# Half-size products for six of eleven tile pairs in a feed-forward, and one list of products with factors made ahead

## The chip, the cores and the metric

The kernel runs on one core of one Trainium2 chip. The metric is the device time of one execution in microseconds (us). A core has TensorE (PE in the profile, with its weight loads as a row PEld of their own), VectorE (DVE), ScalarE (ACT), GpSimd (POOL) and SyncE (SP), which here issues the DMAs of the weights. Each engine takes its instructions in order and waits for others by semaphores.

## The reference

Two layers on 512 tokens of width 1024: differential attention in the first, sliding-window attention with sinks in the second, and in each a feed-forward with a gate (hidden width 2816):

```python
def swiglu(h, w_gate_up, w_down):
    g, u = jnp.split(h @ w_gate_up, 2, axis=-1)
    return (jax.nn.silu(g) * u) @ w_down
...
        x = x + swiglu(rms_norm(x, ffn_norm[l]), w_gate_up[l], w_down[l])
```

Inputs, weights and the result are float32.

## The kernel before

**Numbers in two parts.** TensorE multiplies a rounded format at full rate. Each factor is therefore split into a rounded part `hi` (a ScalarE copy) and the rest `lo` (a VectorE subtraction), and each product is three matmuls, hi x hi, hi x lo and lo x hi (`mm3`, L283 to L286; L585 in the down projection). Splits of gate and up weights are lines L262 and L263, those of the down weights L566 and L567; they land in rings of 8 buffers of 512 columns (`HLB`).

**The feed-forward** (class `Ffn`) holds tokens as columns: the transposed, normalized input `hT` is [128, 8 blocks, 512 tokens], again in two parts. The hidden width is cut into 11 tiles of 256 (`q`), each with a gate half and an up half of two inner tiles of 128. `start` does tile 0 in two halves of 256 tokens, since tokens 256 to 511 are transposed only then. `up(q)` does the others: four accumulations (two inner tiles, gate and up) over 8 blocks, 96 matmuls of 512 columns. `gate` applies silu and multiplies; `left` forms four sums of the gated tile and splits all seven left factors.

**The down projection** already uses seven products instead of eight: over the two halves of tokens, of inner tiles and of output columns. `right` forms four sums of a tile's down weights; `down` takes 2 or 3 tiles (chunks (0,1), (2,3,4), (5,6,7), (8,9,10)) and runs 7 products x 2 blocks of 128 tokens x tiles x 3 matmuls of 512 columns. After each product VectorE adds its bank to `xs`, the residual (L594).

**Order.** PE's order is the program's. For ScalarE, VectorE and SP a planner sets a fixed order when the kernel is built: it goes through time with estimated durations and takes, of what is ready, the first by priority, which is the place in the program, moved forward inside `tc.high_priority(offset=...)`. A tile of a ring can be written only when its last reader is done. SBUF is shared by pools: attention (`da`, `sw`) and feed-forward (`ffn0`, `ffn1`) take turns on the same space, and a tile of the later pool waits for the tiles of the earlier one under it. PSUM has eight banks of 512 columns: four `acc`, three `tr`, one `po`.

## Time and profile before

| what | us |
| --- | --- |
| median of three runs | 1165.65 (1164.84 to 1165.97) |
| the profiled execution, its own time | 1164.51 |
| its span, first to last instruction | 1162.6 |
| PE busy in the span | 1136.0 |
| VectorE busy | 841.5 |
| ScalarE busy | 583.9 |

In the lines of the profile a row names the kernel's line, the engine, the operation and output<-inputs by the program's names. Groups give the count, the total busy time and the mean of one in ns; a timeline gives start and duration in us, with the idle time before in brackets and what ended it; a table by stage gives, for a stretch of the span, each engine's busy time and number of instructions, then the granted TensorE clock, the share of time that the DMA engines were busy, and GB/s.

### The profile page before, as it was taken

To read this page: it belongs to the slowest core of one execution; us is meant where nothing else is said; L and a number is where in the kernel's file an instruction comes from. 1 tells how busy PE (TensorE), PEld (TensorE's weight loads), DVE (VectorE), ACT (ScalarE), POOL (GpSimd) and SP (SyncE) were. 2 spreads that over 40 slices of the span, in tenths; PEclk is the share of its full clock that TensorE was granted. 3 is DMA by queue.
4 is the path that set the end of the run, shared out by engine and by line. 5 is a ranking of instruction groups with operands and counts; after the bars stand their busy time and mean duration, and the time that the engine had idled before them with its cause. 6 is when DMAs were issued, how large, how long until landed. Compare 5 with 4: busy or idle time off the path is not lost.

```text
span 1162.6 us, 16451 instructions
## 1 busy us (share of the span) xinstructions
PE 1136.0 (98%) x5942; PEld 952.5 (82%) x5942; DVE 841.5 (72%) x2052; ACT 583.9 (50%) x1211; POOL 16.5 (1%) x32
## 2 busy tenths in 40 slices
PE   8999999999999999999999999989999999999998
PEld 6878888779888888888888888768988888888887
DVE  5979798978785486476467797987777567468546
ACT  6565756544433343343346579787443343343332
POOL 0100000000000000000002000000000000000000
PEclk9999999999999999999999999999999999999999
DMA  6312112124343134215203221021605206205301
GB/s 191 109 55 74 55 56 67 44 73 158 97 128 126 37 117 146 64 54 182 91 1 94 73 74 55 19 73 34 220 12 188 91 1 217 91 18 181 109 1 73
DMA packets 86579, 103.15 MB, mean 89 GB/s; under 512 B 5161, under 2 KB 68034, under 8 KB 86498
## 3 DMA queue, kind: packets, MB, share of 16 engines
q1 hardware_dynamic: 86064, 100.97, 27.2%
q0 software_dynamic: 384, 1.11, 0.4%
q8 instruction: 47, 0.77, 0.3%
q14 instruction: 34, 0.28, 0.1%
q10 hardware_dynamic: 50, 0.01, 0.0%
HBM read 99.98 MB, written 2.10 MB: 88 GB/s over the span
## 4 chain that ended last, share of the span: by engine, by line
PE 78%; DVE 14%; ACT 5%; DMA 2%; issue 1%; SPq 0%; DVEq 0%; ACTq 0%
PE acc L284 18%; PE acc L286 18%; PE acc L285 18%; PE acc L585 15%; PE tr L585 3%; DVE lo L263 1%; ACT s L1124 1%; DVE hss L377 1%; DVE s L799 1%; PE tr L795 1%; DVE u L393 1%; ACT s L1131 1%; PE po L285 1%; PE tr L302 1%; DMA raw<-in_da_w_qkv_dram 1%
## 5 line engine op out<-in xcount | busy, mean ns | idle before, releaser
L284 PE MATMUL acc<-hTh,hi 128*128 128x512 f32 (+1 forms) x768 | 285.5, 372 | 0.0
L285 PE MATMUL acc<-hTl,hi 128*128 128x512 f32 (+1 forms) x768 | 285.3, 371 | 0.0
L286 PE MATMUL acc<-hTh,lo 128*128 128x512 f32 (+1 forms) x768 | 285.1, 371 | 0.0
L262 ACT CAST hi<-raw 128x512 fp32r<-128x512 f32 x256 | 154.6, 620 | 256.3 <-PE acc L285 119.2
L263 DVE TENSOR_TENSOR lo<-raw,hi 128x512 fp32r<-128x512 f32 x256 | 172.6, 686 | 100.9 <-ACT hi L262 100.7
L566 ACT CAST hi<-g 128x512 fp32r<-128x512 f32 x154 | 95.6, 622 | 160.9 <-PE acc L285 99.4
L285 PEld LDWEIGHTS acc<-hTl,hi 128*128 128x128 f32 x768 | 144.7, 188 | 25.3 <-DVE hTl L291 0.2
L284 PEld LDWEIGHTS acc<-hTh,hi 128*128 128x128 f32 x768 | 144.6, 188 | 24.9
L286 PEld LDWEIGHTS acc<-hTh,lo 128*128 128x128 f32 x768 | 144.6, 188 | 24.9
L567 DVE TENSOR_TENSOR lo<-g,hi 128x512 fp32r<-128x512 f32 x154 | 104.6, 688 | 70.7 <-ACT hi L566 70.7
L284 PE MATMUL acc<-hi,hTh 128*128 128x256 f32 (+1 forms) x384 | 137.5, 358 | 4.9 <-ACT hTh L290 1.6
L286 PE MATMUL acc<-hi,hTl 128*128 128x256 f32 (+1 forms) x384 | 130.1, 339 | 0.3 <-DVE hTl L291 0.2
L285 PE MATMUL acc<-lo,hTh 128*128 128x256 f32 (+1 forms) x384 | 129.6, 337 | 0.4 <-DVE lo L263 0.4
L585 PE MATMUL acc<-hi,al 128*128 128x512 f32 x264 | 103.0, 390 | 0.1
L585 PE MATMUL acc<-hi,ah 128*128 128x512 f32 x264 | 102.9, 390 | 0.0
L585 PE MATMUL acc<-lo,ah 128*128 128x512 f32 x264 | 102.7, 389 | 0.0
L284 PEld LDWEIGHTS acc<-hi,hTh 128*128 128x128 f32 x384 | 72.9, 190 | 15.7 <-issue 3.7
L286 PEld LDWEIGHTS acc<-hi,hTl 128*128 128x128 f32 x384 | 72.7, 189 | 9.4 <-DVE hTl L640 0.7
L285 PEld LDWEIGHTS acc<-lo,hTh 128*128 128x128 f32 x384 | 73.0, 190 | 5.7 <-DVE lo L263 0.7
L594 DVE TENSOR_TENSOR xs<-xs,acc 128x512 f32<-128x512 f32 (+1 forms) x98 | 65.6, 671 | 8.1 <-PE acc L585 6.4
L505 DVE TENSOR_TENSOR sg<-sg,acc 128x512 f32<-128x512 f32 x44 | 30.1, 685 | 53.3 <-PE acc L286 53.3
L585 PEld LDWEIGHTS acc<-hi,al 128*128 128x128 f32 x264 | 49.5, 188 | 11.1 <-DVE al L523 0.9
(210 smaller groups left out, 1784.7 us busy)
## 6 DMA issues: line engine op xcount, KB each, us to landing
raw<-in_w_gate_up_dram SPq DMA_DIRECT2D x88, 512.0 KB, 3.5
g<-in_w_down_dram SPq DMA_DIRECT2D x88, 256.0 KB, 5.1
raw<-in_da_w_qkv_dram SPq DMA_DIRECT2D x30, 256.0 KB, 3.0
raw<-in_da_w_qkv_dram SPq DMA_DIRECT2D x8, 512.0 KB, 3.5
raw<-in_da_w_o_dram SPq DMA_DIRECT2D x8, 512.0 KB, 3.6
raw<-in_sw_w_q_dram SPq DMA_DIRECT2D x8, 512.0 KB, 3.5
raw<-in_sw_w_o_dram SPq DMA_DIRECT2D x8, 512.0 KB, 3.5
raw<-in_w_kv_dram SPq DMA_DIRECT2D x4, 512.0 KB, 3.7
```

What stands on the lines that cost most here:

```text
L262: nc.scalar.copy(hi, part)
L263: nc.vector.tensor_tensor(lo, part, hi.bitcast(F32), op=ALU.subtract)
L284: nc.tensor.matmul(dst, sh, mh, start=start, stop=False)
L285: nc.tensor.matmul(dst, sh, ml, start=False, stop=False)
L286: nc.tensor.matmul(dst, sl, mh, start=False, stop=stop)
L302: nc.tensor.transpose(pt[:, j * P:(j + 1) * P], src[:, k * P:(k + 1) * P], ident)
L377: nc.vector.tensor_reduce(out=ss[:, t, :], in_=sq.rearrange("p (g e) -> p g e", e=HD), axis=AX.X, op=ALU.add)
L505: nc.vector.tensor_tensor(sg, sg, pu, op=ALU.mult)
L566: nc.scalar.copy(hi, src)
L567: nc.vector.tensor_tensor(lo, src, hi.bitcast(F32), op=ALU.subtract)
L585: nc.tensor.matmul(bank[t], l[:, left, tk], r, start=fresh and i == 0 and n == 0, stop=i == len(qs) - 1 and n == 2, skip_group_check=not f ...
L594: nc.vector.tensor_tensor(xs[:, tok, cs], xs[:, tok, cs], bank[t][:, c0:c0 + w], op=ALU.add)
```

## The change

Six tiles (`FAST`: 2, 3, 5, 6, 8, 9) get their gate and up halves from seven half-size products each (`up7`), over the halves of the contraction (blocks 0 to 3 and 4 to 7), of the tokens and of the inner tiles. A product is 4 blocks x 3 matmuls of 256 columns, once for gate and once for up. Four sums of weights per tile are formed on VectorE (`sums12` and two more in `make`), four sums of token blocks once per layer (`tokens`). Banks are read while they go on accumulating: ScalarE copies a partial sum out, VectorE adds later ones to it.

All of a feed-forward after `start` is one list of steps (`Flow`). Each step names the split factors that it uses; a factor is written into the program four places before the step that needs it (`AHEAD`), for `up`, `up7` and `down` alike. The left factors are no longer split as a whole in `left`: seven pairs of 256 columns a tile come from a ring of five (`ah`, `al`). The right sums are formed in place beside the split of the first two right factors. Gate and up weights are loaded into three buffers of 1 MB in the feed-forward's pool (`r`) rather than into the two of 512 KB that all stages share (`raw`), which now hold the weight sums. The rotary tables `Cd` and `Sd` move from the constants' pool to that of the first attention, and the pads of the feed-forward pools go.

```diff
--- before.py
+++ after.py
+FAST = (2, 3, 5, 6, 8, 9)
+AHEAD = {'w': 4, 'a': 4}
+AHB = 5
+WRAW = 3
+XDB = 0
...
+    class Flow:
+        def __init__(self, rings):
+            self.size = rings
+            self.preps, self.steps, self.last = [], [], []
+            self.rings = {r: [] for r in rings}
+        def prep(self, ring, fn, after=-1):
+            order = self.rings[ring]
+            held = order[-self.size[ring]] if len(order) >= self.size[ring] else None
+            order.append(len(self.preps))
+            self.preps.append((fn, held, after))
+            self.last.append(None)
+            return ring, len(order) - 1
+        def step(self, fn, *uses):
+            for ring, k in uses:
+                self.last[self.rings[ring][k]] = len(self.steps)
+            self.steps.append((fn, uses))
+            return len(self.steps) - 1
+        def run(self):
+            made, goal = {r: 0 for r in self.rings}, {r: -1 for r in self.rings}
+            for i, (fn, uses) in enumerate(self.steps):
+                for ring, k in uses:
+                    goal[ring] = max(goal[ring], k + AHEAD[ring])
+                for ring, order in self.rings.items():
+                    while made[ring] < len(order) and made[ring] <= goal[ring]:
+                        make, held, after = self.preps[order[made[ring]]]
+                        if held is not None and (self.last[held] is None or self.last[held] >= i) or after >= i:
+                            break
+                        make()
+                        made[ring] += 1
+                assert all(k < made[ring] for ring, k in uses)
+                fn()
...
+        def gate(self, dst, pg, pu):
+            with tc.high_priority(offset=HOT):
+                nc.scalar.activation(dst, pg, AF.Silu)
+                nc.vector.tensor_tensor(dst, dst, pu, op=ALU.mult)
...
+        def left(self, q):
+            z = self.lf[q]
             tt = nc.vector.tensor_tensor
...
+            tt(z[:, 4, :], z[:, 1, :], z[:, 3, :], op=ALU.add)
+            tt(z[:, 5, :], z[:, 4, :], z[:, 0, :], op=ALU.subtract)
+            tt(z[:, 1, :], z[:, 0, :], z[:, 1, :], op=ALU.subtract)
+            tt(z[:, 6, :], z[:, 2, :], z[:, 5, :], op=ALU.subtract)
+        def load_g(self, q):
+            g = self.gs[q] = self.fp.tile([P, 5, 512], F32, name=nm("g"), tag="g", bufs=3)
             for r in range(2):
                 w = self.wd[:, 2 * q + r, :]
                 nc.sync.dma_start(out=g[:, r, :], in_=w[:, 512:1024])
...
+        def load_r(self, q, j):
+            if q < NQ:
+                r = self.rs[q, j] = self.fp.tile([P, 2, 4, 256], F32, name=nm("r"), tag="r", bufs=WRAW)
+                for c in range(2):
+                    nc.sync.dma_start(out=r[:, c], in_=self.wu[:, 4 * j:4 * j + 4, c * FFN + q * 256:c * FFN + (q + 1) * 256])
+        def split(self, src, shape):
+            hi = wp.tile(shape, F32R, name=nm("hi"), tag="hi", bufs=HLB)
+            lo = wp.tile(shape, F32R, name=nm("lo"), tag="lo", bufs=HLB)
+            nc.scalar.copy(hi, src)
+            nc.vector.tensor_tensor(lo, src, hi.bitcast(F32), op=ALU.subtract)
+            return hi, lo
...
+        def tokens(self):
+            fp, (hh, hl) = self.fp, self.hT
+            self.th, self.tl = (fp.tile([P, 4, 4, 256], F32R, name=nm(z), tag=z) for z in ("th", "tl"))
+            ra, rb = (fp.tile([P, 10, 256], F32, name=nm("g"), tag="g", bufs=3) for _ in range(2))
+            b11, b12, b21, b22 = ra[:, 0:4], ra[:, 4:8], rb[:, 0:4], rb[:, 4:8]
+            tt = nc.vector.tensor_tensor
+            def whole(dst, k, t):
+                sl = (slice(None), slice(k, k + 4), slice(t, t + 256))
+                tt(dst, hh[sl].bitcast(F32), hl[sl].bitcast(F32), op=ALU.add)
+            def put(n, src):
+                nc.scalar.copy(self.th[:, n], src)
+                tt(self.tl[:, n], src, self.th[:, n].bitcast(F32), op=ALU.subtract)
+            whole(b11, 0, 0)
+            whole(b12, 0, 256)
+            whole(b22, 4, 256)
+            whole(b21, 4, 0)
+            tt(b22, b22, b12, op=ALU.subtract)
+            tt(b12, b12, b11, op=ALU.subtract)
+            tt(b11, b22, b11, op=ALU.add)
+            put(0, b12)
+            put(1, b11)
+            tt(b21, b21, b11, op=ALU.subtract)
+            put(2, b22)
+            put(3, b21)
...
+        def up(self, flow, q):
+            parts, banks = {}, []
+            def make(m, c, j):
+                def go():
+                    parts[m, c, j] = self.split(self.rs[q, j][:, c, :, m * P:(m + 1) * P], [P, 4, P])
+                    if m and c:
+                        self.load_r(q + 1 + j, 1 - j)
+                        if j:
+                            self.load_g(q)
+                return go
+            def part(m, c, j):
+                def go():
+                    if j == 0:
+                        banks.append(acc())
+                    hi, lo = parts[m, c, j]
+                    for k in range(4):
+                        z = 4 * j + k
+                        mm3(banks[-1], hi[:, k, :], lo[:, k, :], self.hT[0][:, z, :], self.hT[1][:, z, :],
+                            z == 0, z == KT - 1)
...
+        def up7(self, flow, q):
+            parts, st, bank = {}, {}, {}
+            tt = nc.vector.tensor_tensor
+            def sums12():
+                r0, r1 = self.rs[q, 0], self.rs[q, 1]
+                for n in range(2):
+                    st[n] = wp.tile([P, 2, 4, P], F32, name=nm("raw"), tag="raw", bufs=RAWB)
+                tt(st[0], r0[:, :, :, P:256], r1[:, :, :, P:256], op=ALU.add)
+                tt(st[1], st[0], r0[:, :, :, 0:P], op=ALU.subtract)
...
+                    parts[f, c] = self.split(source(f, c), [P, 4, P])
+                    r0, r1 = self.rs[q, 0], self.rs[q, 1]
+                    if (f, c) == ("11", 1):
+                        sums12()
+                    if (f, c) == ("s1", 1):
+                        tt(r0[:, :, :, P:256], r0[:, :, :, 0:P], r0[:, :, :, P:256], op=ALU.subtract)
+                    if (f, c) == ("s2", 1):
+                        tt(st[0], r1[:, :, :, 0:P], st[1], op=ALU.subtract)
+                    if (f, c) == ("s3", 1):
+                        self.load_r(q + 1, 1)
+                    if (f, c) == ("22", 1):
+                        self.load_r(q + 2, 0)
+                        self.load_g(q)
+                return go
+            def product(f, c, b, n, fresh):
+                def go():
+                    if fresh:
+                        bank[b, c] = acc() if b == "X" else att("po") if (b, c) == ("Z", 1) else att()
+                    hi, lo = parts[f, c]
+                    bh, bl = self.block(n)
+                    dst = bank[b, c][:, 0:256]
+                    for k in range(4):
+                        for i, (l, r) in enumerate(((hi, bh), (hi, bl), (lo, bh))):
+                            nc.tensor.matmul(dst, l[:, k, :], r[:, k, :], start=fresh and k == 0 and i == 0,
+                                             stop=k == 3 and i == 2, skip_group_check=not fresh)
...
+                        if f == "11":
+                            nc.scalar.copy(uc[:, 0, :] if c else lf[:, 0, :], x)
+                        if f == "s1":
+                            nc.scalar.copy(uc[:, 2, :] if c else lf[:, 3, :], y)
+                        if f == "s2":
+                            nc.scalar.copy(uc[:, 1, :] if c else lf[:, 1, :], x)
+                        if f == "12":
+                            d = uc[:, 0, :] if c else lf[:, 0, :]
+                            tt(d, d, z, op=ALU.add)
+                            if c:
+                                tt(lf[:, 0, :], lf[:, 0, :], d, op=ALU.mult)
+                            else:
+                                nc.scalar.activation(d, d, AF.Silu)
+                        if f == "s3":
+                            d = uc[:, 2, :] if c else lf[:, 3, :]
+                            tt(d, d, x, op=ALU.add)
...
+            for f, c in (("11", 0), ("11", 1), ("s1", 0), ("s1", 1), ("s2", 0), ("s2", 1), ("12", 0), ("s3", 0),
+                         ("s3", 1), ("12", 1), ("s4", 0), ("s4", 1), ("22", 0), ("22", 1)):
+                b, n, fresh = {"11": ("X", 0, True), "s1": ("Y", 3, True), "s2": ("X", 4, False), "12": ("Z", 1, True),
+                               "s3": ("X", 5, False), "s4": ("Y", 2, False), "22": ("X", 6, False)}[f]
+                last = flow.step(product(f, c, b, n, fresh), flow.prep("w", make(f, c)))
+            self.ready[q] = last
+        def down(self, flow, qs, last, hook, done):
+            banks, rights, lefts = {}, {}, {}
+            tt = nc.vector.tensor_tensor
+            def make_right(s, q):
+                def go():
+                    g = self.gs[q]
+                    rights[s, q] = [z[:, 0, :] for z in self.split(g[:, (0, 1, 4, 0, 2, 3, 1)[s]:][:, 0:1, :], [P, 1, 512])]
+                    if s == 0:
+                        tt(g[:, 0, :], g[:, 2, :], g[:, 0, :], op=ALU.subtract)
+                        tt(g[:, 4, :], g[:, 3, :], g[:, 0, :], op=ALU.subtract)
+                        tt(g[:, 2, :], g[:, 3, :], g[:, 2, :], op=ALU.subtract)
+                    if s == 1:
+                        tt(g[:, 1, :], g[:, 1, :], g[:, 4, :], op=ALU.subtract)
+                return go
+            def make_left(s, q):
+                def go():
+                    src = self.lf[q][:, (0, 2, 5, 4, 1, 6, 3)[s], :]
+                    ah = self.fp.tile([P, 256], F32R, name=nm("ah"), tag="ah", bufs=AHB)
+                    al = self.fp.tile([P, 256], F32R, name=nm("al"), tag="al", bufs=AHB)
+                    nc.scalar.copy(ah, src)
+                    tt(al, src, ah.bitcast(F32), op=ALU.subtract)
+                    lefts[s, q] = ah, al
+                return go
...
+                uses = [(flow.prep("w", make_right(s, q)), flow.prep("a", make_left(s, q), self.ready[q])) for q in qs]
+                for t in range(2):
+                    for i in range(len(qs)):
+                        flow.step(part(s, b, t, i, fresh, post), *uses[i])
             if "end" in hook:
-                hook["end"]()
+                flow.step(hook["end"])
...
+            self.lf, self.gs, self.rs, self.ready = {}, {}, {}, {0: -1}
+            for q, j in ((1, 0), (1, 1), (2, 0)):
+                self.load_r(q, j)
+            if FAST:
+                self.tokens()
+            flow = Flow({"w": HLB, "a": AHB})
+            flow.step(lambda: self.first_pair())
+            self.ready[0] = 0
             chunks = [(0, 1), (2, 3, 4), (5, 6, 7), (8, 9, 10)]
             for qs in chunks:
                 for q in qs:
                     if q:
-                        self.up(q)
-                    self.gs[q] = self.right(q)
+                        (self.up7 if q in FAST else self.up)(flow, q)
                 end = qs is chunks[-1]
-                self.down(qs, end and ("out" if out else "mid"), hook if end else {}, done)
+                self.down(flow, qs, end and ("out" if out else "mid"), hook if end else {}, done)
+            flow.run()
```

More of the change, by code (lines that the diff above doesn't have):

```diff
@@ L570, in down @@
-        def down(self, qs, last, hook, done):
-            gs = [self.gs[q] for q in qs]
-            parts = [[self.factor(g, 0) for g in gs]]
-            X, Y, Z = ([f() for _ in range(2)] for f in (acc, acc, att))
-            def product(bank, left, s, fresh, post, lead=None):
-                for t in range(2):
-                    if lead and t in lead:
-                        lead[t]()
-                    tk = slice(t * P, (t + 1) * P)
-                    for i, q in enumerate(qs):
-                        ah, al = self.acts[q]
-                        hi, lo = parts[s][i]
-                        mm = ((ah, hi), (ah, lo), (al, hi))
-                        for n, (l, r) in enumerate(mm):
-                            nc.tensor.matmul(bank[t], l[:, left, tk], r, start=fresh and i == 0 and n == 0,
-                                             stop=i == len(qs) - 1 and n == 2, skip_group_check=not fresh)
+        def tokens(self):
[22 more added lines that the diff above has]
+            put(3, b21)
@@ new lines, in block @@
+        def block(self, n):
+            if n < 3:
+                k, t = ((0, 0), (4, 0), (4, 256))[n]
+                return [z[:, k:k + 4, t:t + 256] for z in self.hT]
+            return self.th[:, n - 3], self.tl[:, n - 3]
+        def up(self, flow, q):
[17 more added lines that the diff above has]
+                            z == 0, z == KT - 1)
+                    if c and j:
+                        lf = self.new_lf(q) if m == 0 else self.lf[q]
+                        self.gate(lf[:, 2 * m:2 * m + 2].rearrange("p a q -> p (a q)"), *banks[-2:])
+                        if m:
+                            self.left(q)
+                return go
+            for m in range(2):
+                for c in range(2):
+                    for j in range(2):
+                        last = flow.step(part(m, c, j), flow.prep("w", make(m, c, j)))
+            self.ready[q] = last
@@ L593, in product @@
                             with tc.high_priority(offset=HOT):
-                                nc.vector.tensor_tensor(xs[:, tok, cs], xs[:, tok, cs], bank[t][:, c0:c0 + w], op=ALU.add)
+                                if last or not XDB:
+                                    tt(xs[:, tok, cs], xs[:, tok, cs], bank[:, c0:c0 + w], op=ALU.add)
+                                else:
+                                    xd = self.fp.tile([P, 512], F32, name=nm("xd"), tag="xd", bufs=XDB)
+                                    nc.scalar.copy(xd, bank)
+                                    nc.gpsimd.dma_start(out=xs[:, tok, cs], in_=xd, accum_op=ALU.add)
@@ L595, in product @@
                             if end and last:
                                 done(tok, cs)
[L599 to L610 removed]
+                return go
@@ L611, in down @@
             if "end" in hook:
-                hook["end"]()
+                flow.step(hook["end"])
         def rest(self, fp, hook, done, out=False):
             self.fp = fp
-            self.acts, self.gs = {}, {}
-            sg = [self.gate(self.pts[2 * m], self.pts[2 * m + 1]) for m in range(2)]
-            self.acts[0] = self.left(*sg)
+            self.lf, self.gs, self.rs, self.ready = {}, {}, {}, {0: -1}
+            for q, j in ((1, 0), (1, 1), (2, 0)):
+                self.load_r(q, j)
@@ L990, in tile_yoco_hybrid @@
     with tc.tile_pool(name="ffn0", bufs=1, reuse_waits="tile") as fp:
-        fp.tile([P, 608], F32, name="pad")
         nxt = {}
```

126 lines of the change are left out of this document (66 added, 60 removed).

## The prediction

> **What bounds the kernel now.** I began with the page: its span, the engines' shares and the chain of waits.
>
> ```profile
> span 1162.6 us, 16451 instructions
> PE 1136.0 (98%) x5942; PEld 952.5 (82%) x5942; DVE 841.5 (72%) x2052; ACT 583.9 (50%) x1211; POOL 16.5 (1%) x32
> ...
> PE 78%; DVE 14%; ACT 5%; DMA 2%; issue 1%; SPq 0%; DVEq 0%; ACTq 0%
> PE acc L284 18%; PE acc L286 18%; PE acc L285 18%; PE acc L585 15%; PE tr L585 3%; DVE lo L263 1%; ACT s L1124 1%; DVE hss L377 1%; DVE s L799 1%; PE tr L795 1%; DVE u L393 1%; ACT s L1131 1%; PE po L285 1%; PE tr L302 1%; DMA raw<-in_da_w_qkv_dram 1%
> ```
>
> The chain is TensorE, and the lines that fill it (L284 to L286, L585) are mostly feed-forward. Busy time of PE is modelled, so I looked next at busy time by stage in the first feed-forward: end of `start`, `up(1)`, `down` of tiles 0 and 1, `up` of 2 to 4, their `down`, the last `down` with the hand-over, and, as a check, the three `up` of the second layer.
>
> ```profile
> core 0: us, PE busy (x) PEld busy (x) DVE busy (x) ACT busy (x) POOL busy (x), PEclk, DMA share, GB/s
> 284.50:299.20 14.70, 14.70 (x125) 14.70 (x124) 11.21 (x20) 7.17 (x12) 0.00 (x0) 1.00 0.80 281
> 299.20:320.90 21.70, 21.70 (x98) 17.98 (x97) 13.03 (x23) 8.37 (x14) 0.00 (x0) 1.00 0.17 50
> 320.90:340.30 19.40, 19.37 (x86) 15.72 (x85) 18.77 (x31) 8.32 (x13) 0.00 (x0) 1.00 0.31 94
> 340.30:405.60 65.30, 65.30 (x290) 54.07 (x289) 34.20 (x57) 23.72 (x40) 0.00 (x0) 1.00 0.32 102
> 405.60:434.20 28.60, 28.60 (x128) 23.68 (x127) 24.26 (x40) 12.68 (x20) 0.00 (x0) 1.00 0.31 102
> ...
> 593.30:628.00 34.70, 32.83 (x157) 27.01 (x157) 28.92 (x49) 20.94 (x38) 4.22 (x7) 1.00 0.18 48
> ...
> 877.10:942.40 65.30, 65.30 (x290) 54.07 (x289) 34.27 (x57) 23.83 (x40) 0.00 (x0) 1.00 0.32 101
> ```
>
> PE never pauses at a granted clock of 1.00, so in the feed-forward only cheaper PE work can shorten the time. VectorE is half idle in `up` (34.20 of 65.30) and nearly full in `down` (24.26 of 28.60; 18.77 of 19.40 for two tiles). That imbalance is what the change plays with.
>
> **What a half-size product costs.** Starts of matmuls matter, not their 0.28 or 0.39 us. The 256-wide ones of `start`, first and last of an unbroken stretch, and a 512-wide one after them:
>
> ```profile
> 285.09 0.28 PE L286 MATMUL acc<-hTh,lo 128*128 128x256 f32 x1
> ...
> 299.12 0.28 PE L286 MATMUL acc<-hTh,lo 128*128 128x256 f32 x1
> ...
> 299.71 0.39 PE L286 MATMUL acc<-hTh,lo 128*128 128x512 f32 x1
> ```
> ```profile
> 285.00:299.00 14.00, 14.00 (x120) 1.00 0.80 280
> ```
>
> Lines L284, L285, L286 take turns between them, 117 steps in 14.03 us: 0.120 us each. The 512-wide ones: 65.30 us hold 288 (three `up` of 96; the row's 290 count both edges), 0.2267 each. An `up` of 96 is 21.76 us; `up7` has 7 products x 2 halves x 4 blocks x 3 = 168 matmuls of 256, or 20.16. **Gain: 1.60 us a tile, 19.2 for the twelve** (six a layer), 7% of an `up` and not the eighth that seven for eight suggests, since a half costs 0.53 of a whole. Bounds: the 14.00 us of the second row held at most 120 starts, and at least 116 if four began before it; so 0.117 to 0.121, which gives 25.2 to 17.2 us.
>
> The Trainium skill (TensorE: Matmul & The Clock Gate, "Back-to-back issue gap") speaks against this change: its sustained spacing is 81 ns for 128 columns and 131 ns for 512. An estimate by that page, drawn straight between them, is 98 ns for 256, so 16.5 us for an `up7` against 12.6 for an `up`, and twelve would lose 47 us. The rows here have 120 and 227 ns, and the measurement decides. Rival (5) is this rule's side, worked out from rows.
>
> **What VectorE gets to do.** Its strict cost is again from start to start:
>
> ```profile
> 302.00 0.42 DVE L514 TENSOR_TENSOR ss<-sg,sg 128x256 f32<-128x256 f32 x1
> 302.34 0.68 DVE L523 TENSOR_TENSOR al<-sg,ah 128x512 fp32r<-128x512 f32 x1
> 302.94 0.42 DVE L515 TENSOR_TENSOR ss<-ss,sg 128x256 f32<-128x256 f32 x1
> 303.28 0.68 DVE L567 TENSOR_TENSOR lo<-g,hi 128x512 fp32r<-128x512 f32 x1
> ...
> 305.42 1.23 DVE L523 TENSOR_TENSOR al<-ss,ah 128x1024 fp32r<-128x1024 f32 x1
> 306.56 0.68 DVE L567 TENSOR_TENSOR lo<-g,hi 128x512 fp32r<-128x512 f32 x1
> ```
>
> So 0.34 us for 256 elements, 0.60 for 512, 1.14 for 1024. A fast tile in its `up7`: 14 splits (8.4), four weight sums of 1024 (4.6), six adds out of PSUM, two products of 256 and one of 512 (3.3), `left` (1.4): 17.7 us under 20.2 of PE. A plain `up`: 8 splits, 2 gates, `left`: 7.4 under 21.8. The casts of `left` move into `down` as 7 `al` of 256 a tile, and `right`'s four sums go there as well. A `down` of three tiles then holds 21 `lo` (12.6), 12 sums (7.2), 21 `al` (7.1) and 14 adds to `xs` (8.4), and the last tile's gate and `left` fall into it (2.0): **37.3 us under 28.6 of PE**. Over a chunk of two fast tiles and a plain one that is 2 x 17.7 + 7.4 + 35.3 = 78.1 of 90.6 us (before 34.20 + 24.26 of 93.9). It fits on the whole and not in `down`, so it depends on how far VectorE may run ahead. Four rows tell that:
>
> ```profile
> 288.05 0.69 DVE L535 TENSOR_TENSOR g<-g 128x512 f32<-128x512 f32 x1 [1.53 <-DMA g<-in_w_down_dram]
> ...
> 318.94 0.69 DVE L567 TENSOR_TENSOR lo<-g,hi 128x512 fp32r<-128x512 f32 x1 [2.03 <-ACT hi L566]
> 321.23 0.69 DVE L505 TENSOR_TENSOR sg<-sg,acc 128x512 f32<-128x512 f32 x1 [1.60 <-PE acc L286]
> ```
> ```profile
> ACT hi L566 <- PE acc L285: 99.4, 60, 2.2
> ```
>
> `right`'s sum runs at 288, although `right` is written after the gate, and factors of `down` are made up to 318.94, before its first product at 321. They stop when the eight `hi`/`lo` buffers are full: then `hi` waits for PE, in the `up` of L285. I expect the same of the list: seven factors (4.2), the sums (7.2) and four `al` (1.4) are made during the plain `up`, which leaves 24.5, and the next tile's four splits and first two weight sums (4.7) come to it: 29.2 for 28.6. The 0.6 too much is passed on to an `up7` with 2.5 spare. I take 0.2 us for each of the four inner `down`; bounds 0 and 2.5 (the last tile's `left` and its sums on the path).
>
> **The first chunk** has no cheaper product and gets `tokens`: 12 operations of 1024 (13.7), a little more `al` (14 x 0.34 less 2 x 2.08: 0.6) and the next tile's first weight sums (2.3), less one sum of tile 2 (0.6) that was made there. The rows of before add up to 11.21 + 13.03 + 18.77 = 43.0 of 55.8 us; now it is 59.0, 3.2 too much. Of these I take 2.5 as lost in each layer, since one split of the next tile is not needed at once; bounds 0 and 6 (nothing of `tokens` starts before the last transposes). **Hand-over** to the sliding-window stage: 28.92 of 34.70, plus 21 `al` less 4 made ahead and less 1.7 of before's casts, is 33.0; taken 0.5, bounds 0 and 3.
>
> **Costed at nothing.** ScalarE, by these rows 0.37 us for a copy from PSUM behind at most one cast of 1.05, has two steps of 1.44 us before the bank is added to again:
>
> ```profile
> L522 ACT CAST ah<-ss 128x1024 fp32r<-128x1024 f32 x22 | 23.1, 1049 | 5.3 <-DVE ss L517 5.3
> ...
> L290 ACT CAST aT<-tr 128x256 fp32r<-128x256 f32 x32 | 11.7, 370 | 10.1 <-PE tr L836 7.7 <-DVE aT L291 2.1
> ```
> ```profile
> raw<-in_w_gate_up_dram SPq DMA_DIRECT2D x88, 512.0 KB, 3.5
> g<-in_w_down_dram SPq DMA_DIRECT2D x88, 256.0 KB, 5.1
> ```
>
> ```profile
> 284.31 0.71 PE L302 MATMUL tr<-ident,xn 128*128 128x128 f32 x5
> ```
>
> The DMAs stay as many and as large; 3 MB in the 29.7 us of a fast tile (20.2, and its third of a `down`) is 106 GB/s, and 281 ran in a row above. New is that gate and up weights land in the stage's own pool, so the first wait for the attention's tiles, of which the last (`xn`) are read by the transposes of this row; two loads of 3.5 us are covered by the 14.7 of `start`, and cost up to 7 without it. Queued on SP behind a load that waits for its buffer are only later loads of the same tiles; `g` of tile 1 waits for `tokens` to give its buffer back, some 20 us ahead of its use. The tables moved to the attention's pool change no instruction.
>
> **The sum**, against the profiled execution (1164.51, span 1162.6): -19.2 + 2 x 2.5 + 4 x 0.2 + 0.5 = -12.9, so 1151.6. The median shown, 1165.65, lies 1.1 above that execution, which gives **1152.7 us**.
>
> **Rivals.** (1) *PE loses nothing*: all backlogs fit, 1165.65 - 19.2 = 1146.5. For it: PE paused 0.03 us with VectorE at 18.77 of 19.40. Against: the first chunk's sum is over its time. (2) *Slower: `down` becomes VectorE's.* If factors come only four ahead, as the list is written, then four `lo` (2.4) and ten sums (6.0) are early, no `al`: 28.9 plus the next 4.7 is 33.6 for 28.6, short by 5.0, of which the next `up7` takes 2.5 back. Six `down` at 2.5, two of two tiles at 4.4 (8.4 + 4.8 + 4.8 + 8.4 + 2.0, less 7.2 early, plus 4.7, against 19.0, less 2.5) and the 5.0 of the first chunks are 28.8 against 19.2: 1175. It decides from 2.4 us lost per `down`. Against it stand the rows at 288 and 318.94. (3) *Half of it lost to order*: VectorE's queue is fixed in advance, and in `up7` an operation that waits for a product holds up the splits behind it; one split too late (0.69) in each fast tile is 8.3 more, 1161. For it: rows such as the one at 321.23, where VectorE idles 1.60 us for PE. (4) *No gain*: a half costs 0.1295 (21.76 / 168), or (3) at half again its price: 1165. (5) *A half is not half-priced*: if a matmul held the array in the ratio of the records' durations, 0.28 to 0.39, a half would cost 0.163, an `up7` 27.4, 5.6 more than an `up`, and the time 1233. Against it are the 117 steps of 0.120.
>
> **Chances.** Forecast 0.54 (own range 1147.5 to 1158), (1) 0.14, (3) 0.08, (4) 0.11, (2) 0.12, (5) 0.01. Faster by over 0.2% (0.2% is about what a measurement here can tell from none, 2.3 us) is the forecast, (1) and (3): 0.76; same 0.11; slower 0.13. The range runs from 1145, just under (1), since the average of 117 steps leaves little room for the bound of 0.117, to 1165, which takes in (3) and half of (4) and leaves (2) out.
>
> **What would show it.** An `up7` of 20.2 us in starts of PE, with VectorE near 17.7. A `down` of 28.6 with VectorE full. If waits of weight loads for `lo` or `al` sum to over 10 us, I was wrong about running ahead, and (2) holds if they sit in `down`; in the first chunk I expect the 41.1 us from `up(1)` to the end of its `down` to become about 43.5. A spacing of the half-size matmuls above 0.121 would break the first term.

## The result and the profile after

The changed kernel takes 1151.43 us (median of 4 runs, 1150.19 to 1151.75) beside 1165.81 for the kernel before: a ratio of 0.9871, with a 95% interval of 0.9859 to 0.9883. The forecast was 1152.7. The profiled execution took 1150.19 us with a span of 1148.1, against 1164.51 and 1162.6, so the spans differ by 14.4 us.

The page of the kernel after, its shares and its chain of waits:

```profile
span 1148.1 us, 18912 instructions
...
PE 1123.8 (98%) x6806; PEld 979.7 (85%) x6806; DVE 995.2 (87%) x2368; ACT 659.4 (57%) x1463; POOL 20.4 (2%) x32
...
PE 76%; DVE 16%; ACT 4%; DMA 2%; issue 1%; SPq 0%; DVEq 0%; ACTq 0%
PE acc L706 12%; PE acc L289 10%; PE acc L291 10%; PE acc L290 10%; PE tr L791 9%; PE acc L791 8%; PE tr L706 7%; DVE lo L268 2%; PE po L706 1%; DVE s L1024 1%; DVE hss L382 1%; PE po L791 1%; PE po L290 1%; PE tr L1020 1%; DVE xs L460 1%
```

TensorE still sets the end, and VectorE went from 72% to 87% of a shorter span without taking the chain over. L706 is the product of `up7`, L791 that of `down`. Busy time by stage, in the first layer: `up(1)`, `down` of tiles 0 and 1, the two `up7` of tiles 2 and 3, the plain `up` of tile 4, and their `down`:

```profile
core 0: us, PE busy (x) PEld busy (x) DVE busy (x) ACT busy (x) POOL busy (x), PEclk, DMA share, GB/s
299.30:321.70 22.40, 22.16 (x99) 17.99 (x98) 22.35 (x36) 7.62 (x16) 0.00 (x0) 1.00 0.59 188
321.70:341.70 20.00, 19.70 (x85) 15.69 (x84) 19.37 (x38) 11.54 (x25) 0.00 (x0) 1.00 0.19 61
341.70:381.80 40.10, 40.10 (x338) 40.07 (x337) 36.26 (x65) 24.00 (x49) 0.00 (x0) 1.00 0.41 128
381.80:403.60 21.80, 21.80 (x99) 18.01 (x98) 18.83 (x32) 6.99 (x13) 0.00 (x0) 1.00 0.31 97
403.60:432.90 29.30, 29.30 (x128) 23.77 (x127) 28.53 (x55) 16.86 (x37) 0.00 (x0) 1.00 0.30 102
```

From the starts of PE the two `up7` take 40.05 us for 336 matmuls, the plain `up` 21.81, the `down` 29.27. Before, three `up` took 65.28 and a `down` 28.56. The same starts, stage by stage through the whole span, give this account (us):

| part | forecast | measured |
|---|---|---|
| twelve fast tiles (six stretches of 65.28, now 61.86) | -19.2 | -20.5 |
| `up(1)` and the first `down`, both layers (41.15, now 42.46 and 42.43) | +5.0 | +2.6 |
| four inner `down` (28.56, now 29.27 or 29.28) | +0.8 | +2.9 |
| the rest | +0.5 | +0.6 |
| sum | -12.9 | -14.4 |

The rest is +0.28 up to and in the `start` parts, +0.61 in the last `down` of layer one, +0.79 from the last `up` to the end, and the stage between the two feed-forwards, which became 1.05 shorter. Its rows, before and then after:

```profile
617.84:811.29 193.45, 180.97 (x1099) 155.69 (x1098) 160.53 (x524) 150.43 (x393) 8.59 (x16) 1.00 0.18 59
```
```profile
610.97:803.37 192.40, 182.32 (x1099) 157.11 (x1098) 160.21 (x526) 149.93 (x393) 1.13 (x2) 0.99 0.18 59
```

The line that asks for an explanation is the inner `down`: 0.7 us longer, with PE busy throughout. VectorE is at 28.53 of 29.30, which the prediction had as 29.2 of work for 28.6, "0.6 too much", so a VectorE that is late would fit well. But late factors show as waits, and these are all the waits of weight loads for `al` and, in `up(1)`, for `lo`, in the whole feed-forward:

```profile
PEld tr L791 <- DVE al L775: 1.5, 2, 0.7
...
PEld acc L291 <- DVE lo L579: 1.3, 2, 0.7
```

Two waits each, all four in the first chunks of the two layers. In the inner `down` there is none. There each matmul starts a little later than before (0.23 or 0.24 us after the one ahead, 29.27 / 126 = 0.2323 on average; before 28.56 / 126 = 0.2267). PE's timeline in that `down`:

```profile
403.83 0.40 PE L791 MATMUL tr<-lo,ah 128*128 128x512 f32 x1
404.06 0.39 PE L791 MATMUL tr<-hi,al 128*128 128x512 f32 x1
404.29 0.39 PE L791 MATMUL tr<-hi,ah 128*128 128x512 f32 x1
404.52 0.39 PE L791 MATMUL tr<-lo,ah 128*128 128x512 f32 x1
```

A matmul of the same form, granted clock 1.00, no wait, 5.6 ns slower. What else is different is where the operands lie. The diff takes the 608-element pad out of the feed-forward's pools, and with it every tile of these pools now starts 128 bytes past a multiple of 256 in its partition (addresses of the built kernels: `ah` at 126976 bytes before, a multiple of 256, and at 213632 after, 128 bytes past one). The factors `hi` and `lo`, in a pool of their own, and the tokens `hTh` and `hTl` still start on such a multiple. In a record such as `tr<-hi,ah`, `hi` is the side that streams (the data) and `ah` the weights.

### The profile page after: what moved, and what is told of

Its sections match the earlier page's. It is cut to its first block, busy times and chain, and to the rows that moved or that the text cites. A ratio compares the mean times of both kernels' runs of the same rounds, so it can differ in the third digit from the quotient of the medians.

```text
span 1148.1 us, 18912 instructions
## 1 busy us (share of the span) xinstructions
PE 1123.8 (98%) x6806; PEld 979.7 (85%) x6806; DVE 995.2 (87%) x2368; ACT 659.4 (57%) x1463; POOL 20.4 (2%) x32
## 4 chain that ended last, share of the span: by engine, by line
PE 76%; DVE 16%; ACT 4%; DMA 2%; issue 1%; SPq 0%; DVEq 0%; ACTq 0%
PE acc L706 12%; PE acc L289 10%; PE acc L291 10%; PE acc L290 10%; PE tr L791 9%; PE acc L791 8%; PE tr L706 7%; DVE lo L268 2%; PE po L706 1%; DVE s L1024 1%; DVE hss L382 1%; PE po L791 1%; PE po L290 1%; PE tr L1020 1%; DVE xs L460 1%
## 5 line engine op out<-in xcount | busy, mean ns | idle before, releaser
L578 ACT CAST hi<-g 128x512 fp32r<-128x512 f32 x154 | 95.2, 618 | 113.1 <-PE acc L290 104.4
L578 ACT CAST hi<-r 128x512 fp32r<-128x512 f32 x160 | 98.6, 620 | 75.5 <-PE acc L706 44.2
L291 PE MATMUL acc<-hTh,lo 128*128 128x512 f32 (+1 forms) x384 | 136.4, 355 | 0.7 <-DVE lo L579 0.5
L289 PE MATMUL acc<-hTh,hi 128*128 128x512 f32 (+1 forms) x384 | 136.2, 355 | 0.0
L290 PE MATMUL acc<-hTl,hi 128*128 128x512 f32 (+1 forms) x384 | 136.1, 354 | 0.0
L579 DVE TENSOR_TENSOR lo<-r,hi 128x512 fp32r<-128x512 f32 x160 | 106.2, 690 | 18.4 <-ACT hi L578 18.0
L579 DVE TENSOR_TENSOR lo<-g,hi 128x512 fp32r<-128x512 f32 x154 | 105.5, 691 | 12.6 <-ACT hi L578 12.2
L267 ACT CAST hi<-raw 128x512 fp32r<-128x512 f32 x96 | 57.4, 618 | 43.8 <-PE acc L291 26.8
L706 PE MATMUL acc<-th,hi 128*128 128x256 f32 x288 | 81.1, 282 | 0.0
L706 PE MATMUL acc<-tl,hi 128*128 128x256 f32 x288 | 81.1, 282 | 0.0
L706 PE MATMUL acc<-th,lo 128*128 128x256 f32 x288 | 81.0, 281 | 0.0
L268 DVE TENSOR_TENSOR lo<-raw,hi 128x512 fp32r<-128x512 f32 x96 | 64.6, 687 | 10.0 <-ACT hi L267 9.9
```

Source lines behind the costliest of these rows:

```text
L267: nc.scalar.copy(hi, part)
L268: nc.vector.tensor_tensor(lo, part, hi.bitcast(F32), op=ALU.subtract)
L289: nc.tensor.matmul(dst, sh, mh, start=start, stop=False)
L290: nc.tensor.matmul(dst, sh, ml, start=False, stop=False)
L291: nc.tensor.matmul(dst, sl, mh, start=False, stop=stop)
L578: nc.scalar.copy(hi, src)
```

## The experiments

Theory A, at first: a weight operand that starts off the multiple costs 5.6 ns in each 512-wide matmul. The rival, which the prediction would have chosen, is that VectorE is late. A second question is whether the list of products does anything by itself, and a third how much room VectorE had left.

**The kernel before, with its tiles moved by 128 bytes.**

```diff
-        fp.tile([P, 608], F32, name="pad")
+        fp.tile([P, 512], F32, name="pad")
```

(in both feed-forward pools)

> The kernel before, its feed-forward pads 512 instead of 608 elements wide: nothing else changes, but all tiles of the feed-forward pools start 384 bytes lower, at 128 past a multiple of 512 bytes instead of on one, as they do in the changed kernel. Theory A (the slower matmuls of the new down stage, 0.2323 us for 0.2267, come from where the left factors lie): each three-tile down goes from 28.56 to 29.27 us, the two-tile ones by 0.47, the up stages stay at 65.28; about 5.2 us slower, 1171. Theory B (they come from the list: more waits per product, or VectorE writing while PE reads): no change, 1165.8.

Measured: 1172.07 (1170.65 to 1174.15) beside 1167.35, ratio 1.0048 [1.0036, 1.0061]. Three `up`, then `down`:

```profile
340.65:405.96 65.31, 65.31 (x290) 54.05 (x288) 34.12 (x57) 23.85 (x40) 0.00 (x0) 1.00 0.32 98
405.96:435.23 29.27, 29.27 (x127) 23.73 (x126) 25.22 (x41) 12.65 (x20) 0.00 (x0) 1.00 0.33 105
```

The `down` has the 29.27 us of the kernel after with none of its change, and VectorE is at 25.22 of it. VectorE is not the cause.

**The kernel after, with its tiles back on the multiple**, all of them:

```diff
     with tc.tile_pool(name="ffn0", bufs=1, reuse_waits="tile") as fp:
+        fp.tile([P, 96], F32, name="pad")
```

(and the same in the second)

> The changed kernel with 96 elements of padding at the start of both feed-forward pools, so that all its tiles start on multiples of 512 bytes again. Theory A: three-tile down 28.56 us, two-tile ones 0.47 shorter, and the products of the token sums th and tl return from 0.1188 to 0.120 us a matmul (up7 from 20.02 to 20.16): -5.2 + 1.6, about 1147.8. Theory B: 1151.4, down stays at 29.27.

**The kernel after, with only the tiles behind `left`'s buffers moved**, so that `ah` and `al` (and `uc`) start on the multiple and `th`, `tl` of the half-size products don't:

```diff
+            self.fp.tile([P, 96], F32, name="pad")
```

> The changed kernel with the same padding placed behind lf, so that only ah, al and uc move onto multiples of 512 bytes; r, th, tl, g and lf stay 128 past them. Theory A, if it is the weight side that matters: down 28.56 and up7 still 20.02, about 1146.2, the fastest of all. If it is the data side of some other tile: as the changed kernel, 1151.4. Theory B: 1151.4.

Measured: all tiles moved, 1148.61 (1148.24 to 1149.14), ratio 0.9844 [0.983, 0.9857]; only those behind `left`, **1146.51 (1145.63 to 1146.81), ratio 0.9824 [0.9811, 0.9838]**, which is quicker than both kernels. The two `up7`, the `up` and the `down`, first with all moved, then with those behind `left`:

```profile
342.14:382.45 40.31, 40.31 (x337) 40.31 (x336) 36.24 (x65) 23.98 (x49) 0.00 (x0) 1.00 0.41 131
382.45:404.24 21.79, 21.79 (x99) 18.03 (x97) 18.83 (x32) 6.99 (x13) 0.00 (x0) 1.00 0.30 97
404.24:432.80 28.56, 28.56 (x128) 23.65 (x126) 28.23 (x55) 16.82 (x37) 0.00 (x0) 1.00 0.29 98
```
```profile
340.90:380.90 40.00, 40.00 (x337) 40.00 (x336) 36.17 (x64) 23.97 (x49) 0.00 (x0) 1.00 0.43 131
380.90:402.70 21.80, 21.80 (x98) 18.05 (x97) 18.88 (x32) 6.99 (x13) 0.00 (x0) 1.00 0.30 97
402.70:431.30 28.60, 28.60 (x128) 23.65 (x127) 28.24 (x55) 16.81 (x37) 0.00 (x0) 1.00 0.29 101
```

In both, `down` is back at 28.56 from start to start with VectorE at 28.2: it carries 99% and costs PE nothing. The half-size products go the other way. With `th` and `tl` on the multiple they take 40.31 / 336 = 0.1200 us each, which is the number of the prediction, and with them off it 40.05 / 336 = 0.1192.

**A multiple of 256, or of 512?** The kernel before with pads of 544 elements, `ah` and `al` at 256 past a multiple of 512:

```diff
-        fp.tile([P, 608], F32, name="pad")
+        fp.tile([P, 544], F32, name="pad")
```

> The kernel before with feed-forward pads of 544 elements: ah and al start 256 past a multiple of 512 bytes, so each weight row of 512 bytes still crosses such a multiple, but starts on a multiple of 256. If crossing a multiple of 512 is what costs: down 29.27 us, 1171. If starting off a multiple of 256 is: down 28.56, 1165.8.

Measured: 1167.06 (1165.15 to 1168.6) beside 1166.62, ratio 1.0004 [0.9995, 1.0013], with a `down` as before the change:

```profile
406.32:434.88 28.56, 28.56 (x127) 23.65 (x126) 24.37 (x40) 12.68 (x20) 0.00 (x0) 1.00 0.32 104
```

A multiple of 256 is enough. And with pads of 496, 64 bytes past it:

> The kernel before with the tiles of the feed-forward 64 bytes past a multiple of 256 (pads of 496 elements). Theory A (a start off a multiple of 256 costs, however far off): `down` of three tiles 29.27 us, of two 19.8, and the time some 6 us above before, as with 128 bytes. Rival (the price goes by how many bytes of the first row lie outside): `down` at 64 bytes differs from 29.27, between 28.56 and 30.0. Rival (only 128 is bad): 28.56.

Measured: 1172.4 (1171.86 to 1172.65) beside 1166.66, ratio 1.0049 [1.0026, 1.0072], and a `down` of

```profile
405.57:434.97 29.40, 29.40 (x127) 23.69 (x126) 25.00 (x41) 12.82 (x21) 0.00 (x0) 1.00 0.33 106
```

29.40 / 126 = 0.2333: as bad as 128 bytes, or 1 ns worse.

**Is it the weight side?** So far only that side had been moved under 512-wide products. Three runs of the kernel before move the others, with pads that leave every other tile of the feed-forward where it was past a multiple of 512. First the factors `hi` and `lo`, which are the weights in `up` and the data in `down`:

```diff
+    wp.tile([P, 32], F32, name="pad")
-    sp.tile([P, 16], F32, name="pad")
+    sp.tile([P, 112], F32, name="pad")
...
-        fp.tile([P, 608], F32, name="pad")
+        fp.tile([P, 480], F32, name="pad")
```

> The kernel before with the factors hi and lo of all weights moved by 128 bytes (they start 128 bytes past a multiple of 512), and the tiles of the feed-forward left where they were. In `up` these factors are the weight side of the matmuls, in `down` the data side, and in `start` the data side of the 256-wide ones. Theory A (only the weight side pays, 232.3 in place of 226.7 ns): three `up` take 65.28 + 288 x 0.0056 = 66.9 us, `up(1)` 22.3, while `down` stays at 28.56 and the 256-wide part of `start` at 14.47; the feed-forward alone adds 2 x 960 x 0.0056 = 10.8 us. Rival (either side pays): `down` goes to 29.27 or above as well. Rival (it was something else about the tiles of `left`, their place against the other tiles and not their start): all stages stay as before, and the time within 0.2% of it.

Measured: 1184.47 (1182.2 to 1186.73) beside 1166.66, ratio 1.0156 [1.0107, 1.0205]. Three `up`, then `down`:

```profile
341.33:408.52 67.19, 67.19 (x290) 54.05 (x288) 34.20 (x57) 23.80 (x40) 0.00 (x0) 1.00 0.30 96
408.52:437.92 29.40, 29.40 (x128) 23.65 (x127) 24.88 (x41) 12.87 (x21) 0.00 (x0) 1.00 0.33 106
```

Theory A falls: the `down` pays as well, with its weights where they always were and its data moved. Either each operand pays for its own start, or what counts is the distance between the two. Then the tokens, data in `up`:

```diff
+    wp.tile([P, 96], F32, name="pad")
...
     xs = xp.tile([P, NT, D], F32, name="xs")
+    xp.tile([P, 32], F32, name="pad")
...
-        fp.tile([P, 608], F32, name="pad")
+        fp.tile([P, 480], F32, name="pad")
```

> The kernel before with only the tokens (hTh, hTl) moved by 128 bytes, all else on the starts it had. In `up` the tokens are the data side of the 512-wide matmuls, in `start` the weight side of 256-wide ones; `down` does not read them. Theory B (in a 512-wide product either side pays, some 6 to 7 ns a matmul): three `up` 66.9 to 67.2 us, `down` 28.56, and the time some 11 us above before for the feed-forward alone, more with the attention's products. Theory A (weight side only): three `up` 65.28, `start` above 14.47 (120 x 5.6 ns: 15.1). What 256-wide products pay for a weight side off its start is open: 14.3 to 15.2.

And `hi`, `lo` with the feed-forward's tiles, all at 128, so that in `down` both sides are off by the same:

```diff
+    wp.tile([P, 32], F32, name="pad")
-    sp.tile([P, 16], F32, name="pad")
+    sp.tile([P, 112], F32, name="pad")
...
-        fp.tile([P, 608], F32, name="pad")
+        fp.tile([P, 512], F32, name="pad")
```

> The kernel before with the factors hi and lo of the weights and the tiles of the feed-forward all 128 bytes past a multiple of 256: in `down` both sides are off by the same. Theory B (each operand pays for its own start): `down` of three tiles at least 29.4 us, up to 30.3 if the prices add. Rival R (it is the distance of the two operands that counts): `down` back at 28.56, while the `up`, whose tokens stay on their start, keep 67.2.

Measured: tokens, 1179.1 (1178.61 to 1179.6) beside 1166.22, ratio 1.0113 [1.0082, 1.0143]; both, 1180.07 (1178.5 to 1181.64), ratio 1.0121 [1.0078, 1.0164]. Three `up` and `down`, first of the run with the tokens moved, then of that with both:

```profile
340.48:407.67 67.19, 67.19 (x289) 54.06 (x288) 34.19 (x57) 23.80 (x40) 0.00 (x0) 1.00 0.31 97
407.67:436.25 28.58, 28.58 (x128) 23.66 (x126) 24.37 (x40) 12.68 (x20) 0.00 (x0) 1.00 0.31 100
```
```profile
340.86:408.05 67.19, 67.19 (x289) 54.06 (x288) 34.14 (x57) 23.82 (x40) 0.00 (x0) 1.00 0.30 96
408.05:436.63 28.58, 28.58 (x128) 23.65 (x126) 24.62 (x40) 12.69 (x20) 0.00 (x0) 1.00 0.32 102
```

This is rival R. In `down`, where weights and data are off by the same, a matmul is back at 28.57 / 126 = 0.2267; in `up`, where they differ by 128 bytes, 67.19 / 288 = 0.2333 (the `up` stages hold 6 x 1.91 + 0.52 + 0.61 = 12.6 of the 14.0 us between the spans of the profiled executions). With the tokens alone moved, `up` pays the same 67.19 us and `down`, which doesn't read them, stays. So in these unbroken stretches it is the **distance between the starts of the two operands, counted past multiples of 256 bytes**: 0 (in three ways: none moved, both moved by 128, one by 256) gives 226.7 ns for a 512-wide matmul; 64 or 128 gives 232.3 to 233.3.

For the 256-wide products the sign is the other. The 120 of `start` take 14.47 us with their two sides alike, and 14.31 to 14.33 in the three runs that put them apart. Its rows, in the kernel before and with the tokens moved:

```profile
284.77:299.24 14.47, 14.47 (x124) 14.47 (x122) 11.25 (x20) 7.01 (x12) 0.00 (x0) 1.00 0.79 279
```
```profile
284.48:298.79 14.31, 14.31 (x123) 14.31 (x122) 11.14 (x19) 7.00 (x12) 0.00 (x0) 1.00 0.81 280
```

The half-size products of `up7` start 120.0 ns apart with all tiles on the multiple. The 119.2 of the kernel after is a mean: four of the seven products read `th` or `tl` and come 118.8 ns apart, the other three read `hTh` and `hTl`, whose start did not move, and come 119.7 apart. Why the distance matters, and why the two widths differ in sign, was not shown. The third run above has the best of both: equal starts under the 512-wide products of `down`, and unequal ones under the products of `th` and `tl`.

The Trainium skill (TensorE: Matmul & The Clock Gate, "Step-by-step: what each phase is for") says that TensorE reads weights and streamed data through two independent ports, so that loading the next weights takes no read bandwidth from the running matmul. That names no reason for which the distance should matter, and here it is worth 2.5 to 2.9% of a 512-wide product; no run here shows by which path.

**The list alone.** The kernel after with no fast tile, so that `tokens` and `up7` are gone and the order of the list stays:

```diff
-FAST = (2, 3, 5, 6, 8, 9)
+FAST = ()
```

> The changed kernel with no fast tile: the list of products, its rings and its loads alone, no half-size products and no token sums. If the half-size products carry the whole gain and the list costs only the slower matmuls of down: all up stages 21.8 us, down 29.27, the first chunk without its stalls (0.5 in up(1), 0.6 in its down), 1165.8 + 5.2 = 1171. If making factors ahead had a gain of its own: below 1165.8.

Measured: 1170.58 (1170.08 to 1172.0) beside 1167.35, ratio 1.0031 [1.0019, 1.0043]. The first `down` (two tiles), the three `up`, and their `down`:

```profile
321.74:341.85 20.11, 19.81 (x85) 15.76 (x84) 19.40 (x38) 11.61 (x25) 0.00 (x0) 1.00 0.19 55
341.85:407.18 65.33, 65.33 (x289) 54.05 (x288) 35.28 (x61) 19.90 (x36) 0.00 (x0) 1.00 0.35 112
407.18:436.46 29.28, 29.28 (x128) 23.74 (x126) 27.77 (x54) 16.82 (x37) 0.00 (x0) 1.00 0.29 94
```

The list gains nothing by itself: the `up` are as before, and the 128 bytes are paid. What it costs beyond them is 0.36 us in the first `down` of a layer, where the `al` of the first tile are late (20.11 here; 19.73 in the quickest kernel, which has the list and the address put right; 19.37 before). `up(1)` takes 21.79 here against 22.37 with `tokens`, so `tokens` costs 0.58. This run is 1.5 us quicker than the first experiment, which has the address without the list (1170.58 and 1172.07), but that is not shown to be a gain of the list: in the profiled executions its stage between the two feed-forwards happens to be 2.28 us shorter (192.46 for 194.74), and that stage, taken up below, moves without a cause that was found.

**How far ahead factors must be made.** The list names the step ahead of which a factor is made; without that lead:

```diff
-AHEAD = {'w': 4, 'a': 4}
+AHEAD = {'w': 0, 'a': 0}
```

> The changed kernel with the places that a factor is written ahead of its step set from four to none. Theory A (how far VectorE runs ahead is set by the planner and by the rings of eight and five buffers, not by the place in the list): at most 1 us slower, 1151 to 1152.5. Theory B (the four places are the run-ahead, rival 2 of the prediction): down waits for its first factors and the sums of weights, 10 us or more slower, 1161 and up.

Measured: 1153.99 (1152.48 to 1154.48) beside 1166.62, ratio 0.989 [0.9874, 0.9906]. Two `up7`, `up`, `down`, and the stage between the feed-forwards:

```profile
342.15:382.19 40.04, 40.04 (x337) 40.04 (x336) 36.19 (x64) 23.98 (x49) 0.00 (x0) 1.00 0.42 131
382.19:404.00 21.81, 21.81 (x98) 18.02 (x97) 18.85 (x32) 6.99 (x13) 0.00 (x0) 1.00 0.31 97
404.00:433.28 29.28, 29.28 (x128) 23.74 (x126) 28.47 (x55) 16.82 (x37) 0.00 (x0) 1.00 0.30 102
611.39:806.82 195.43, 182.82 (x1100) 156.99 (x1098) 160.64 (x526) 150.59 (x393) 1.13 (x2) 0.99 0.18 58
```

These stages are the same as in the kernel after to 0.01 us, and the first chunks to 0.05. So the number in the list does not set how far VectorE runs ahead. The waits of the kernel after point to free buffers instead: `hi`, from which a `lo` is made, waits 104.4 us in all for PE's matmuls of a plain `up`, which give its buffers back.

The time lies above theory A's 1152.5 and far below theory B. Of the 3.98 us by which the profiled execution is longer, 3.03 lie in the stage between the feed-forwards (195.43 for 192.40), 0.48 in `start` of layer two and 0.47 ahead of the first `up(1)`; none of this code was touched. That stage moves by 1 to 3 us from kernel to kernel (193.45 before, 192.40 after, 195.43 here, 194.17 in the quickest). The granted clock there was 0.50 in no stretch before, in one of 3.41 us in the kernel after and here, and in two in the quickest, which doesn't put the four in order. What moves the stage stays open; a try is next.

**A pad for the second attention too**, on top of the quickest kernel:

```diff
     with tc.tile_pool(name="sw", bufs=1, reuse_waits="tile") as ap:
+        ap.tile([P, 96], F32, name="pad")
```

> The kernel of e3 with 96 elements of padding at the start of the sliding-window stage's pool as well, so that its oh, ol, q, kT and p tiles start on multiples of 512 bytes. In the trace of before, the output projection there, whose weight side is oh and ol, took 229 to 232 ns a matmul at its quickest. Theory A: 192 matmuls of 0.232 become 0.2267, about 1 us less: 1145.5. If that stage waits for other engines anyway: no change, 1146.5.

Measured: 1147.38 (1146.36 to 1148.01), ratio 0.9836 [0.9822, 0.985]: no gain over 1146.51. The stage takes 193.86 us against 194.17. By the starts of PE the pad does act: of the 192 matmuls there that read `oh` or `ol`, 55 come at most 227 ns apart, against 2 without it. Most of the others still take 230 ns or more at equal starts. They run in groups of a few, between other work, so the 226.7 ns above hold for the unbroken stretches of the feed-forward; why not here was not shown.

**All nine inner tiles fast**, on top of the quickest kernel, so that no plain `up` is left in which VectorE can work ahead:

```diff
-FAST = (2, 3, 5, 6, 8, 9)
+FAST = (2, 3, 4, 5, 6, 7, 8, 9, 10)
```

> The kernel of e3 with nine fast tiles a layer, 2 to 10, instead of six. PE would save 3 x 1.74 us more in each layer, 10.5 in all: 1136 if VectorE's work stays hidden. VectorE, by the sums of the prediction, gets 3 x 17.7 + 35.3 = 88.4 us in a chunk of 3 x 20.0 + 28.6 = 88.6, with no plain up in which to run ahead. Theory A (VectorE is the second limit, and the plain up of each chunk is what pays for down): PE waits for lo or al in every down, at least 1.5 us a chunk, so 1143 or more. Theory B (there is room left): 1136 to 1138.

Measured: 1181.36 (1177.33 to 1183.3) beside 1166.62, ratio 1.0124 [1.0104, 1.0144], slower than before. Three `up7`, then `down`; PE's timeline around the longest wait there; and the waits of weight loads for `al` in all:

```profile
342.20:402.20 60.00, 60.00 (x505) 60.00 (x504) 54.93 (x97) 36.01 (x75) 0.00 (x0) 1.00 0.39 122
402.20:438.30 36.10, 31.26 (x128) 25.34 (x128) 35.43 (x69) 17.18 (x37) 0.00 (x0) 0.91 0.23 76
```
```profile
403.87 0.40 PE L791 MATMUL tr<-lo,ah 128*128 128x512 f32 x1
409.11 0.79 PE L791 MATMUL tr<-hi,al 128*128 128x512 f32 x1 [4.84 <-DVE al L775]
409.70 0.63 PE L791 MATMUL tr<-hi,ah 128*128 128x512 f32 x1
410.12 0.63 PE L791 MATMUL tr<-lo,ah 128*128 128x512 f32 x1
...
414.30 0.39 PE L791 MATMUL tr<-hi,al 128*128 128x512 f32 x1
```
```profile
PEld tr L791 <- DVE al L775: 24.2, 7, 5.8
...
PEld acc L791 <- DVE al L775: 10.5, 10, 3.8
```

And three stretches of that `down`: the pause, what follows it, and the time at half the clock:

```profile
403.87:409.11 5.24, 0.40 (x3) 0.01 (x1) 5.24 (x12) 0.00 (x0) 0.00 (x0) 0.83 0.00 0
409.11:414.20 5.09, 5.09 (x12) 4.03 (x13) 4.71 (x10) 2.85 (x6) 0.00 (x0) 0.50 0.02 5
407.35:414.18 6.83, 5.07 (x12) 4.01 (x13) 6.45 (x15) 2.83 (x6) 0.00 (x0) 0.50 0.02 4
```

The `up7` keep their 20.0 us each. The `down` goes from 28.56 to 36.1 with VectorE at 35.43: rival (2) of the prediction, with nine tiles instead of six. That is 7.5 us, far above the least that my expectation named, 1.5 a chunk. Some 5.0 us of it are one pause (no matmul starts between 403.87 and 409.11, and one was due at 404.10); each of the six `down` has one such pause, of 3.8 to 5.8 us from start to start. VectorE works all through it: it makes five sums of `right`, the four of `left` and a `lo` before the `al` that PE waits for. With six fast tiles all twelve sums of `right` of this chunk run in the plain `up`; here six of them run in the `down`.

After the pause 12 steps take 5.19 us (409.11 to 414.30) instead of 12 x 0.2267 = 2.72, another 2.5 us, and the granted clock there is 0.50. The Trainium skill (TensorE: Matmul & The Clock Gate, "What's actually happening") says that the clock goes to half after an idle window of about 3.4 us, and back after as long a busy one. The first half agrees: the clock fell at 407.35, 3.5 us after the last matmul had started. It came back at 414.18, after 5.1 us of matmuls, which is longer than one such window. So this wait is paid one and a half times over.

## Why the prediction was right, and where it was not

The time, the sign and the engine that bounds the kernel came out as forecast (1152.7 for 1151.43), and the gain comes from the half-size products, as forecast: the list without them takes 1170.58. But two terms of the sum were wrong and nearly cancelled, by luck: the first chunks cost 2.4 us less than forecast, and the inner `down` 2.1 more.

**The gain.** Forecast 19.2 us from 0.120 and 0.2267 us a matmul. With all operands on the same start it is 6 x (65.28 - 40.31 - 21.79) = 19.1, so the step holds to 0.1 us. As built it was 20.5, since `th` and `tl` lie 128 bytes off the factors they meet. The 7% of an `up` was right for equal starts (8% as built), and rival (5) is out: the half-size matmuls start 119 to 120 ns apart. The 98 ns estimated from the Trainium skill (TensorE: Matmul & The Clock Gate, "Back-to-back issue gap") are not borne out either, nor the loss of 47 us by them.

**What VectorE gets to do.** Forecast 29.2 of work in an inner `down` and 35.4 in two `up7`: 28.53 and 36.26 measured. The first pair tests little, since a full engine can't show more work than the stage is long. The account of what runs early is the better test: seven `lo`, the twelve sums and four `al` were to be made during the plain `up`, and in the trace of the kernel after seven `lo` of the down weights, all twelve sums and three `al` start there, two `al` earlier. That it runs ahead whatever the list says is shown by the run without a lead. That it would be full without harm in `down` is shown by the runs with the address put right (28.24 of 28.60, no wait); that the plain `up` is what makes this possible, by the run with nine fast tiles.

**The inner `down`**, the step that failed. I took 0.2 us each for the 0.6 by which VectorE's work was too much, between bounds of 0 and 2.5. VectorE cost 0.0, and the address 0.71. The sum has no term for it: under "Costed at nothing" I went through DMAs, tables and ScalarE, and didn't ask what the two lines that drop a pad do to every tile behind them. In all it costs 4 x 0.71 for the inner `down`, 0.61 and 0.71 for the last ones (108 and 126 matmuls in a row) and 2 x 0.37 for the first: 4.9 us, and the quickest kernel, with that term gone, is 1151.43 - 1146.51 = 4.9 below the kernel after. That the two agree so well is in part chance: the profiled executions lie 3.65 us apart, since the quickest kernel is 1.77 longer in the stage between the feed-forwards and 0.49 shorter ahead of its first `up(1)`. Had I only compared my table with the result, 0.7 found for 0.6 worked out would have passed for a hit.

**The first chunk.** Forecast 2.5 a layer, measured 1.3. Of this 0.37 is the address, 0.36 the list's late `al`, and 0.58 `tokens`; so what I had priced at 2.5, VectorE's 3.2 too much, came to 0.94. It was mis-sized: PE waited for VectorE once in `up(1)` and once in its `down` in each layer, and VectorE worked 41.7 of the 42.4 us of the two rows (22.35 and 19.37), where I had looked at 59.0 us for a stretch of 55.8 with `start` in it.

**Hand-over.** Forecast 0.5. The last `down` of layer one took 0.61 more, which 108 x 5.6 ns explains, and the stage behind it 1.05 less, which nothing in the prediction explains. That the rest came to 0.6 for 0.5 is luck.

**The rivals.** (1), 1146.5, is what the quickest kernel measured, but by coincidence and not for its reason: PE still loses 0.94 us in each first chunk there, and the products gain 20.5 and not 19.2. (2) is a real mechanism, which six fast tiles a layer stay clear of and nine don't. (3) and (4) left no trace: no product in `up7` waits.

## What to carry to other kernels

Half-size products here save 7 to 8% and not 12.5% of an `up`, and they paid only while a stage in front had the spare time in which VectorE makes the next stage's operands; count VectorE over each stretch between places where it can run ahead, not over the whole. When matmuls of one form get slower by a few per cent with no wait beside them, compare the start addresses of their two operands in the partition before looking for a busy engine, and whenever a buffer or a pad is added or dropped, look at what it does to the tiles behind it. A match of one term with its forecast proves its cause only when a run takes that cause away.

## What the runs showed of the hardware that was not expected

- In the unbroken stretches of the feed-forward a 512-wide float32r matmul starts every 226.7 ns if its weights and its data start at the same place past a multiple of 256 bytes in their partition, and every 232.3 to 233.3 ns at distances of 64 and 128 bytes. Either operand may be the one that is moved, and both moved alike cost nothing. Other distances were not tried.
- For 256-wide matmuls it is the other way, and less: they start every 118.8 to 119.4 ns with the two 128 bytes apart, every 119.7 to 120.6 ns with equal starts.
- A pause of 5.0 us was followed by 5.1 us of matmuls at a granted clock of 0.50, which added 2.5 us to it.
